# Down projections of a SwiGLU feed-forward as seven block products, with the block products chained in PSUM banks

## The chip, the cores and the metric

The kernel runs on one core of one Trainium2 chip. The metric is the device time of one execution in microseconds (us), given as the median of several runs. The profile is of one execution.

## The reference

Two layers of a decoder trunk over 512 tokens of 1024 features, all in fp32; the change concerns the feed-forward of both layers, where 2816 hidden features are 22 chunks of 128.

```python
def swiglu_ffn(h, w_gate_up, w_down):
    gu = h @ w_gate_up
    gate, up = gu[..., :D_FF], gu[..., D_FF:]
    return (jax.nn.silu(gate) * up) @ w_down

def reference(...):
    for i in range(DEPTH):                      # DEPTH = 2
        if i % N_MIXERS == 0:
            x = x + dilated_attention_mixer(rmsnorm(x, attn_norm[j]), w_qkv[j], w_attn_out[j])
        else:
            x = x + pooling_mixer(rmsnorm(x, pool_norm[j]), w_pool_in[j], w_pool_group[j], pool_scale[j])
        x = x + swiglu_ffn(rmsnorm(x, ffn_norm[i]), w_ffn_gate_up[i], w_ffn_down[i])
    return rmsnorm(x, final_norm)
```

## The kernel before

**Layout.** The residual stream is held transposed as eight tiles `X[0]` to `X[7]` of 128 features x 512 tokens. A product of a 128x128 weight block with such a tile is a matmul of 512 columns (one PSUM bank); with half the tokens it has 256 columns.

**Precision.** Each fp32 product is three matmuls: an operand is split into a high and a low part (`split`: ACT copies the high part, DVE subtracts it to get the low one), and the kernel adds high x high, high x low and low x high. Lines L254, L255 and L257 are these three in a plain product (class `Product`), L371, L372 and L373 in a block product (`mult`). Weights are split as well: tiles `whi`/`wlo` (or `halfhi`/`halflo`) come from a `raw` tile that a DMA filled, on L77 (ACT) and L78 (DVE).

**Block products.** For 17 of the 22 chunks of a feed-forward, gate and up together are one product of 2x2 blocks: the two block rows of the result are gate and up, the block columns are the two halves of the tokens, and the inner dimension is cut in two. Seven products of blocks stand in for eight (Strassen in Winograd's form), named "11", "1", "2", "21", "3", "22" and "4" after the operand of the tokens; each is 4 times 3 matmuls of 256 columns. Function `seven` runs them, each into a bank half of its own, and DVE adds the parts up (L412, L420, L425, L426). The first five chunks (`NPLAIN`) are plain pairs, while the operands of the tokens (`prepare`, `normed`) are still being made. The sums of weight blocks that a block product needs are made per chunk from three SP loads (L134, L135, L136), an accumulating DMA on POOL's queue (L137) and two DVE additions (L150, L151); class `Pair` does it.

**Down.** A feed-forward goes in two halves of 11 chunks (`HALF`). After each half, eight plain products of 11 chunks, one per output tile `m`, are added to `X[m]` (L954, or L879 in the second half of layer 0, which writes in the token order of layer 1). Their weights are 768 and 640 columns wide (`DOWN`). The last two tiles of layer 1 are made by halves of the tokens (`end`, `add`, `emit`, L1055 to L1072), with the final norm behind.

**Order.** Instructions are issued in the order in which the program writes them. Weights go through queues in the order of use: `loads` (DMAs), `steps` (splits) and `units`; `pump` issues the next of each when a buffer of the rings `BUFS` is free, and is called behind each product. PSUM has eight banks in rotation under one name, `ps`.

Of the kernel before, what the change touches and what calls it, by code (L numbers as in the profile page):

```python
# [15 lines left out]
P = 128  # L16
# [6 lines left out]
HALF = FC // 2  # L23
# [15 lines left out]
DOWN = (6, 5)  # L39
# [3 lines left out]
SLOTS = 15  # L43
# [5 lines left out]
def trunk(ctx: ExitStack, tc: tile.TileContext, xT, norms, w_first, w_qk, w_qkp, w_v0, w_v0p, w_v12, w_out, w_pair, w_down, w_pin, w_pgrp,  # L49
# [5 lines left out]
    psum = ctx.enter_context(tc.tile_pool(name="psum", bufs=8, space=PSUM))  # L55
# [10 lines left out]
    def ps():  # L66
        return psum.tile([P, S], F32, tag="ps", name="ps")


# [51 lines left out]
    class Pair:  # L121
# [3 lines left out]
        def __init__(self, src):  # L125
            self.src, self.w = src, {}
            loads.append((self, {"raw": 2, "rawhalf": 1}, self.load))
# [4 lines left out]
        def load(self):  # L132
            self.a, self.b, self.c = Held("raw"), Held("raw"), Held("rawhalf")
            nc.sync.dma_start(self.b.t, self.src[:, :2 * S])  # L134
            nc.sync.dma_start(self.a.t, self.src[:, S:3 * S])  # L135
            nc.sync.dma_start(self.c.t, self.src[:, :S])  # L136
            nc.gpsimd.dma_start(self.b.t.rearrange("p (a c) -> p a c", a=2),  # L137
                                self.src[:, None, 3 * S:].to_broadcast([P, 2, S]), accum_op=OP.add)

        def blocks(self):  # L140
            self.w["b"] = Held("w")
            split(*self.w["b"].t, self.a.t)

        def sums(self):
            self.w["s"] = Held("w")
            split(*self.w["s"].t, self.b.t)

        def more(self):
            a, b = self.a.t, self.b.t
            nc.vector.tensor_add(a[:, :S], a[:, :S], b[:, :S])  # L150
            nc.vector.tensor_add(a[:, S:], a[:, S:], a[:, :S])  # L151
            self.b.done()
            self.w["m"] = Held("w")
            split(*self.w["m"].t, a)
            self.a.done()

        def last(self):
            self.w["l"] = Held("half")
            split(*self.w["l"].t, self.c.t)
            self.c.done()  # L160
# [44 lines left out]
    def ffn_plan(layer):  # L205
        for hf in range(2):
            for j in range(hf * HALF, (hf + 1) * HALF):
# [4 lines left out]
            for m in range(KC):  # L212
                src = w_down[layer, hf, m]
                plain(src[:, :DOWN[0] * P], src[:, DOWN[0] * P:])
# [11 lines left out]
    class Product:  # L226


        def __init__(self, n, ins, w=None, keep=None):
# [935 lines left out]
```

## Time and profile before

| | us |
|---|---|
| median of 3 runs | 1267.53 (1267.21 to 1268.39) |
| span of the profiled execution | 1264.5 |
| PE busy | 1250.9 (99%), 8382 matmuls |
| PE weight loads | 1156.7 (91%) |
| DVE busy | 926.3 (73%) |
| ACT busy | 571.5 (45%) |
| POOL busy | 130.1 (10%) |

The mean granted TensorE clock is 0.998. The engines are PE (TensorE), PEld (its weight loads), DVE (VectorE), ACT (ScalarE), POOL (GpSimd) and SP (SyncE, which issues DMAs). An L with a number is a line of the program. A row for one instruction has its start from the beginning of the span, its duration, engine, line, operation, tiles (written <- read), shape and, in brackets, how long the engine was idle before it and what released it. A row for a group has a count, busy time and mean duration in ns, then the idle time ahead of the group and what ended it. Matmuls overlap, so their durations add up to more than the time they take.

### The profile page before, as it was taken

To read this page: it belongs to the slowest core of one execution; us is meant where nothing else is said; L and a number is where in the kernel's file an instruction comes from. 1 tells how busy PE (TensorE), PEld (TensorE's weight loads), DVE (VectorE), ACT (ScalarE), POOL (GpSimd) and SP (SyncE) were. 2 spreads that over 40 slices of the span, in tenths; PEclk is the share of its full clock that TensorE was granted. 3 is DMA by queue.
4 is the path that set the end of the run, shared out by engine and by line. 5 is a ranking of instruction groups with operands and counts; after the bars stand their busy time and mean duration, and the time that the engine had idled before them with its cause. 6 is when DMAs were issued, how large, how long until landed. Compare 5 with 4: busy or idle time off the path is not lost.

```text
span 1264.5 us, 21069 instructions
## 1 busy us (share of the span) xinstructions
PE 1250.9 (99%) x8382; PEld 1156.7 (91%) x8382; DVE 926.3 (73%) x1395; ACT 571.5 (45%) x885; POOL 130.1 (10%) x123
## 2 busy tenths in 40 slices
PE   9999999999999999999999999999999999999997
PEld 7889999999999988899989999888789988999987
DVE  6987788878778845689636887558978953788643
ACT  6445554545445543445324554343444532455331
POOL 1011111212111000110001110000301000110000
PEclk9999999999999999999999999999999999999999
DMA  8336556655756433256456774333135645676322
GB/s 295 101 95 164 130 157 145 162 139 144 182 137 152 139 133 120 67 129 181 124 146 158 181 188 126 97 133 130 37 95 123 175 126 142 168 182 173 93 69 67
DMA packets 67875, 174.04 MB, mean 138 GB/s; under 512 B 6960, under 2 KB 9152, under 8 KB 67776
## 3 DMA queue, kind: packets, MB, share of 16 engines
q1 hardware_dynamic: 48816, 136.49, 33.3%
q0 software_dynamic: 17808, 35.14, 16.4%
q8 instruction: 66, 1.08, 0.3%
q10 hardware_dynamic: 1152, 1.05, 0.2%
q14 instruction: 33, 0.27, 0.1%
HBM read 170.56 MB, written 2.10 MB: 137 GB/s over the span
## 4 chain that ended last, share of the span: by engine, by line
PE 75%; issue 12%; DVE 10%; ACT 1%; POOL 1%; DMA 0%; DVEq 0%; POOLq 0%
PE ps L372 13%; PE ps L371 13%; PE ps L373 13%; PE ps L254 8%; PE ps L255 8%; PE ps L257 8%; PE ps L483 2%; PE ps L484 2%; PE ps L485 2%; DVE wlo L78 2%; PE ps L678 1%; PE ps L590 1%; DVE raw L434 1%; POOL rcol L323 1%; PE ps L656 1%
## 5 line engine op out<-in xcount | busy, mean ns | idle before, releaser
L77 ACT ACTIVATE whi<-raw 128x1024 fp32r<-128x1024 f32 (+2 forms) x299 | 298.1, 1002 | 428.2 <-PE ps L255 198.4
L78 DVE TENSOR_TENSOR wlo<-raw,whi 128x1024 fp32r<-128x1024 f32 (+2 forms) x299 | 343.2, 1152 | 158.6 <-ACT whi L77 157.4
L254 PE MATMUL ps<-a,whi 128*128 128x512 f32 (+1 forms) x374 | 141.0, 377 | 0.0
L255 PE MATMUL ps<-a,whi 128*128 128x512 f32 (+1 forms) x374 | 140.9, 377 | 0.0
L257 PE MATMUL ps<-a,wlo 128*128 128x512 f32 (+1 forms) x374 | 140.8, 377 | 0.0
L371 PE MATMUL ps<-tt,whi 128*128 128x256 f32 x408 | 115.5, 283 | 0.0
L372 PE MATMUL ps<-tt,whi 128*128 128x256 f32 x408 | 115.5, 283 | 0.0
L373 PE MATMUL ps<-tt,wlo 128*128 128x256 f32 x408 | 115.5, 283 | 0.0
L137 POOL DMA_DIRECT2D raw<-w_pair x34 | 41.1, 1209 | 440.8 <-DMA raw<-w_pair 152.6
L257 PEld LDWEIGHTS ps<-a,wlo 128*128 128x128 f32 x374 | 70.4, 188 | 13.0
L254 PEld LDWEIGHTS ps<-a,whi 128*128 128x128 f32 x374 | 70.4, 188 | 12.8
L255 PEld LDWEIGHTS ps<-a,whi 128*128 128x128 f32 x374 | 70.4, 188 | 12.7
L371 PEld LDWEIGHTS ps<-tt,whi 128*128 128x128 f32 x408 | 78.3, 192 | 0.0
L372 PEld LDWEIGHTS ps<-tt,whi 128*128 128x128 f32 x408 | 78.3, 192 | 0.0
L373 PEld LDWEIGHTS ps<-tt,wlo 128*128 128x128 f32 x408 | 78.3, 192 | 0.0
L372 PE MATMUL ps<-tb,whi 128*128 128x256 f32 x272 | 77.2, 284 | 0.1
L373 PE MATMUL ps<-tb,wlo 128*128 128x256 f32 x272 | 77.0, 283 | 0.0
L371 PE MATMUL ps<-tb,whi 128*128 128x256 f32 x272 | 76.9, 283 | 0.0
L371 PE MATMUL ps<-h,whi 128*128 128x256 f32 x252 | 72.7, 289 | 0.0
L373 PE MATMUL ps<-h,wlo 128*128 128x256 f32 x252 | 71.3, 283 | 0.0
L372 PE MATMUL ps<-h,whi 128*128 128x256 f32 x252 | 71.3, 283 | 0.0
L254 PE MATMUL ps<-h,whi 128*128 128x512 f32 x144 | 56.4, 392 | 0.0
(280 smaller groups left out, 3415.5 us busy)
## 6 DMA issues: line engine op xcount, KB each, us to landing
raw<-w_pair SPq DMA_DIRECT2D x78, 512.0 KB, 4.3
raw<-w_qkp SPq DMA_DIRECT2D x36, 512.0 KB, 4.7
raw<-w_pair POOLq DMA_DIRECT2D x34, 512.0 KB, 7.2
raw<-w_down SPq DMA_DIRECT2D x32, 384.0 KB, 3.1
raw<-w_down SPq DMA_DIRECT2D x32, 320.0 KB, 2.8
raw<-w_v SPq DMA_DIRECT2D x18, 512.0 KB, 3.9
raw<-w_qkp POOLq DMA_DIRECT2D x18, 512.0 KB, 7.3
rawhalf<-w_pair SPq DMA_DIRECT2D x34, 256.0 KB, 3.5
```

The lines of the kernel that those rows point to most:

```text
L77: nc.scalar.activation(hi, v, AF.Copy)
L78: nc.vector.tensor_tensor(lo, v, hi.bitcast(F32), op=OP.subtract)
L137: nc.gpsimd.dma_start(self.b.t.rearrange("p (a c) -> p a c", a=2), self.src[:, None, 3 * S:].to_broadcast([P, 2, S]), accum_op=OP.add)
L254: nc.tensor.matmul(self.p[:, cols], w[0][:, s], mh[:, cols], start=self.done == 0, stop=False)
L255: nc.tensor.matmul(self.p[:, cols], w[0][:, s], ml[:, cols], start=False, stop=False)
L257: nc.tensor.matmul(self.p[:, cols], w[1][:, s], mh[:, cols], start=False, stop=self.done == self.n)
L371: nc.tensor.matmul(dst, w.t[0][:, c], th, start=k == 0, stop=False)
L372: nc.tensor.matmul(dst, w.t[0][:, c], tl, start=False, stop=False)
L373: nc.tensor.matmul(dst, w.t[1][:, c], th, start=False, stop=k == K2 - 1)
L483: nc.tensor.matmul(o, mh, wh, start=k == 0, stop=False)
L484: nc.tensor.matmul(o, mh, wl, start=False, stop=False)
L485: nc.tensor.matmul(o, ml, wh, start=False, stop=k == K2 - 1)
```

## The change

1. **Down as block products.** 20 of the 22 chunks go through down projections made as seven block products, in three groups: after chunks 0 to 7, 8 to 13 and 14 to 19 (`GROUPS`). A group has four of them (`down(g, i)`), one for each pair of output tiles `X[2i]`, `X[2i+1]`. Their products are of 4, 3 and 3 times 3 matmuls of 256 columns. The gate/up work of one more chunk is issued ahead of groups 0 and 1. Their weight blocks come through `Pair`, now for any width, from matrices that the host has cut into blocks (`down_blocks`).
2. **The last two chunks** stay plain products, two output tiles per weight unit (`last_plain`); block products of the last group and plain turns alternate by `TURNS`.
3. **Chains.** All block products of the feed-forwards now run in `chain` and no longer in `seven`: bank c takes "11", then "2", "3" and "4" on top; d starts as a copy of c after "11" and takes "21"; e starts as a copy of c after "2" and takes "22". "1" has a bank of its own. Five callbacks read the results (`share`, `left`, `high`, `right`, `low`). ACT makes the copies (L463, L471).
4. **Blocks of the hidden activation.** `half_of` and `blocks_of` turn the activations of two chunks into seven operands, with subtractions and splits on DVE and ACT (L989, L1004, L1005, L1012), two pieces behind each product of a chain from the fourth on (`some`). `up` is negated where it is written, and the sums into `X` change signs.
5. **Banks.** After the attention the eight banks are 3 `ps`, 3 `seed` (d, e) and 2 `sum` (c); plain products alternate between `ps` and `seed` (`full`). During the attention the three names rotate through all eight. There is one more slot for activations (`SLOTS` 16), and working tiles come from pools of their own.
6. **The end.** In layer 1 the last plain turns, for `X[4]` to `X[7]`, are made by halves of the tokens (L1243, L1248, L1259). The squares for the norms are summed in one tile in place (L306 to L310).

The next rows are DVE's in the first half of layer 0's feed-forward, from one gate/up block product to the next, before (`first` and `sums` are scratch tiles of `seven`, `a` the split activation):

```order
L412 TENSOR_TENSOR gt<-ps,first 128x512
L78 TENSOR_TENSOR wlo<-raw,whi 128x1024 x2
L420 TENSOR_TENSOR sums<-ps,gt 128x512
L78 TENSOR_TENSOR wlo<-raw,whi 128x1024
L425 TENSOR_TENSOR up<-ps,sums 128x512
L426 TENSOR_TENSOR gt<-sums,ps 128x256
L150 TENSOR_TENSOR raw<-raw 128x512
L78 TENSOR_TENSOR halflo<-rawhalf,halfhi 128x512
L866 TENSOR_TENSOR up<-up,gt 128x512
L151 TENSOR_TENSOR raw<-raw 128x512
L78 TENSOR_TENSOR a<-up,a 128x512
```

The same place in the changed kernel, on DVE (`hx` and `t` hold blocks of the hidden activation; L1072 is `high`, L1066 is `right`):

```order
L967 TENSOR_TENSOR hid<-up,gt 128x512
L173 TENSOR_TENSOR raw<-raw 128x512
L97 TENSOR_TENSOR hx<-hid,hx 128x256
L174 TENSOR_TENSOR raw<-raw 128x512
L989 TENSOR_TENSOR t<-hid 128x256
L97 TENSOR_TENSOR halflo<-rawhalf,halfhi 128x512
L97 TENSOR_TENSOR hx<-t,hx 128x256
L97 TENSOR_TENSOR wlo<-raw,whi 128x1024
L1072 TENSOR_TENSOR up<-sum,half 128x256
L97 TENSOR_TENSOR wlo<-raw,whi 128x1024
L1066 TENSOR_TENSOR gt<-seed,half 128x256
L97 TENSOR_TENSOR wlo<-raw,whi 128x1024
```

Four evacuations of up to 512 columns became two of 256, the blocks of the hidden activation came in, and one `wlo` now stands right ahead of `high`.

On DVE in layer 0's first down projections, before, the sums into `x` alternate with weight splits:

```order
L954 TENSOR_TENSOR x<-x,ps 128x512
L78 TENSOR_TENSOR wlo<-raw,whi 128x640
L954 TENSOR_TENSOR x<-x,ps 128x512
L78 TENSOR_TENSOR wlo<-raw,whi 128x768
L78 TENSOR_TENSOR wlo<-raw,whi 128x640
L954 TENSOR_TENSOR x<-x,ps 128x512
```

In the changed kernel DVE has this over one down chain of group 1 in layer 0 (L1080 and L1081 are `share`, L1084 `left`, L1087 `high`, L1085 `right`, L1086 `low`):

```order
L173 TENSOR_TENSOR raw<-raw 128x384
L97 TENSOR_TENSOR halflo<-rawhalf,halfhi 128x384
L1080 TENSOR_TENSOR x<-x,ps 128x256
L1081 TENSOR_TENSOR x<-x,ps 128x256
L174 TENSOR_TENSOR raw<-raw 128x384
L1084 TENSOR_TENSOR x<-x,seed 128x256
L97 TENSOR_TENSOR wlo<-raw,whi 128x768
L1087 TENSOR_TENSOR x<-x,sum 128x256
L97 TENSOR_TENSOR wlo<-raw,whi 128x768
L1085 TENSOR_TENSOR x<-x,seed 128x256
L97 TENSOR_TENSOR wlo<-raw,whi 128x768
L1086 TENSOR_TENSOR x<-x,sum 128x256
```

A chain makes two output tiles with six sums of 256 columns, and the additions for its weight blocks are new here; again a `wlo` stands ahead of `high`.

On PE, the end of a gate/up block product of layer 0 before: "22" into one bank, then "4" into another (bank names with their numbers):

```order
L371 MATMUL ps_6707<-tn_5901,whi_6609 128x256
L372 MATMUL ps_6707<-tn_5901,whi_6609 128x256
L373 MATMUL ps_6707<-tn_5901,wlo_6610 128x256
L371 MATMUL ps_6706<-tt_5749,halfhi_6629 128x256
L372 MATMUL ps_6706<-tt_5749,halfhi_6629 128x256
```

The same place in a down chain of the changed kernel, with sum_8020 this chain's bank c, which "3" wrote and `high` reads, seed_8023 its bank e, and sum_8120 the next chain's c:

```order
L389 MATMUL seed_8023<-hy_7847,whi_7967 128x256
L390 MATMUL seed_8023<-hy_7847,whi_7967 128x256
L391 MATMUL seed_8023<-hy_7847,wlo_7968 128x256
L389 MATMUL sum_8120<-hx_7173,whi_8002 128x256
L389 MATMUL sum_8020<-hu_7332,halfhi_7981 128x256
L390 MATMUL sum_8020<-hu_7332,halfhi_7981 128x256
```

"4" now goes to the bank that "3" had, and one matmul of the next chain stands ahead of it.

The diff, cut to its core:

```diff
-HALF = FC // 2
+GROUPS = ((0, 8), (8, 14), (14, 20))
+LAST = FC - GROUPS[-1][1]
+TURNS = (("block", 0), ("block", 1), ("plain", 0), ("block", 2), ("plain", 1), ("block", 3), ("plain", 2), ("plain", 3))
-DOWN = (6, 5)
-SLOTS = 15
+SLOTS = 16
+RING = ("ps", "seed", "sum", "ps", "seed", "sum", "ps", "seed")
+BANKS = {"ps": 3, "seed": 3, "sum": 2}
...
+    def chain(T, share, left, right, low, high, behind=None):
+        unit, = units.popleft()
+        n = unit.q // P
+        c, a, d, e = (ps(tag)[:, :H2] for tag in ("sum", "ps", "seed", "seed"))
+        ...
+        def step():
+            pump()
+            i = next(turns)
+            if behind:
+                behind(i)
+
+        wb = part(unit, "b")
+        mult(c, wb, 0, T, "11", n=n)
+        nc.scalar.copy(d, c)
+        step()
+        ws = part(unit, "s")
+        mult(a, ws, 0, T, "1", n=n)
+        share(a)
+        step()
+        wm = part(unit, "m")
+        mult(c, wm, 0, T, "2", True, n=n)
+        nc.scalar.copy(e, c)
+        step()
+        mult(d, wb, 1, T, "21", True, n=n)
+        wb.done()
+        left(d)
+        step()
+        mult(c, ws, 1, T, "3", True, n=n)
+        ws.done()
+        high(c)
+        step()
+        mult(e, wm, 1, T, "22", True, n=n)
+        wm.done()
+        right(e)
+        step()
+        wl = part(unit, "l")
+        mult(c, wl, 0, T, "4", True, n=n)
+        wl.done()
+        low(c)
+        step()
...
+            def some(i):
+                for n in range(2 if i > 2 else 0):
+                    if pieces:
+                        pieces.popleft()()
+
+            def strassen_pair(j):
+                ...
+                def right(p):
+                    nc.vector.tensor_sub(gt[:, hi], p, half)
+                    nc.scalar.activation(gt[:, hi], gt[:, hi], AF.Silu)
+
+                chain(T, lambda p: nc.scalar.copy(half, p),
+                      lambda p: nc.scalar.activation(gt[:, lo], p, AF.Silu), right,
+                      lambda p: nc.scalar.copy(up[:, lo], p),
+                      lambda p: nc.vector.tensor_sub(up[:, hi], p, half), some)
+                hide(j, gt, up)
+
+            def down(g, i):
+                x1, x2 = X[2 * i], X[2 * i + 1]
+
+                def share(p):
+                    nc.vector.tensor_add(x1[:, hi], x1[:, hi], p)
+                    nc.vector.tensor_sub(x2[:, hi], x2[:, hi], p)
+
+                chain(TH[g], share,
+                      lambda p: nc.vector.tensor_sub(x1[:, lo], x1[:, lo], p),
+                      lambda p: nc.vector.tensor_sub(x1[:, hi], x1[:, hi], p),
+                      lambda p: nc.vector.tensor_add(x2[:, lo], x2[:, lo], p),
+                      lambda p: nc.vector.tensor_add(x2[:, hi], x2[:, hi], p))
...
-            for hf in range(2):
-                ...
-                for m in range(KC - 2 if nxt == 4 and hf else KC):
-                    ...
-                        nc.vector.tensor_add(X[m], X[m], f.p)
+            for g, (first, stop) in enumerate(GROUPS):
+                for j in range(first + (g > 0), stop + 1 if g < 2 else FC):
+                    if j < NPLAIN:
+                        plain_pair(j)
+                        if j < K2:
+                            prepare(j)
+                    else:
+                        strassen_pair(j)
+                if g < 2:
+                    while len(pieces) > 2:
+                        pieces.popleft()()
+                    for i in range(K2):
+                        down(g, i)
+                    drop("hb")
+            ...
+            for kind, i in TURNS[:-2] if layer else TURNS:
+                if kind == "block":
+                    down(2, i)
+                else:
+                    last_plain(i)
...
+            for m in range(K2, KC):
+                sq = add(m, 0, end(m, 0))
+            add(4, 1, end(4, 1))
+            r = rstd([sums[0], sq])
+            add(5, 1, end(5, 1))
+            add(6, 1, end(6, 1))
+            pr = spread(r)
+            f = end(7, 1)
+            emit(0, pr, range(2))
+            sq = add(7, 1, f)
+            r = rstd([sums[1], sq])
+            ...
+            emit(0, pr, range(2, KC))
+            ...
+            emit(1, pr, range(KC), spare, row)
```

More of the change, by code (lines that the diff above doesn't have):

```diff
@@ L923, in prepare @@
[L923 to L935 removed]
+                T["22", k] = cut(two(T["n"], k % 2), b22)
+                give(("hp", k))
+                give(("tp", k))
@@ L1145 @@
         "w_pair": pair,
-        "w_down": dn,
+        "w_down": down,
+        **{f"w_down{g}": down_blocks(*span) for g, span in enumerate(GROUPS)},
         "w_pin": tiled(v["w_pool_in"][0]),
```

504 lines of the change are left out of this document (285 added, 219 removed).

## Prediction

> **What bounds the kernel now.** I read the page's engine table and slices first, then busy time by stage over the first feed-forward layer, then single instructions in it. The page:
>
> ```profile
> span 1264.5 us, 21069 instructions
> PE 1250.9 (99%) x8382; PEld 1156.7 (91%) x8382; DVE 926.3 (73%) x1395; ACT 571.5 (45%) x885; POOL 130.1 (10%) x123
> ...
> PE   9999999999999999999999999999999999999997
> PEld 7889999999999988899989999888789988999987
> DVE  6987788878778845689636887558978953788643
> ```
>
> TensorE (PE) is busy in every slice but the last, and no other engine is. The stages of layer 0's feed-forward (columns: PE, PEld, DVE, ACT, POOL busy, then granted clock, DMA share and GB/s) are plain pairs, gate/up block products, down projections, gate/up again, a mixed stretch, down projections:
>
> ```profile
> 509.00:553.70 44.70, 44.57 (x200) 36.70 (x200) 38.10 (x58) 20.65 (x31) 4.49 (x3) 1.00 0.33 82
> 553.70:625.00 71.30, 71.25 (x552) 69.19 (x551) 57.35 (x83) 34.00 (x50) 4.82 (x4) 1.00 0.61 162
> 625.00:665.00 40.00, 40.00 (x178) 33.15 (x177) 15.77 (x20) 10.08 (x12) 2.41 (x2) 1.00 0.49 133
> 665.00:760.00 95.00, 95.00 (x757) 93.37 (x756) 77.34 (x104) 47.01 (x61) 10.86 (x9) 1.00 0.68 175
> 760.00:820.00 60.00, 60.00 (x366) 54.01 (x366) 38.44 (x58) 25.11 (x36) 0.00 (x0) 1.00 0.37 114
> 820.00:857.00 37.00, 37.00 (x169) 30.80 (x168) 18.96 (x23) 15.28 (x21) 0.00 (x0) 1.00 0.37 128
> ```
>
> PE never pauses there, at full clock; DVE has 19% free beside block products and 61% in the down stage. So time is the sum of PE's issue intervals, and the change is worth what it takes off them, less every wait it makes. Durations overlap, so I take intervals between starts, 76 of each kind:
>
> ```profile
> 489.81 0.39 PE L255 MATMUL ps<-oh,whi 128*128 128x512 f32 x1
> ...
> 507.03 0.39 PE L257 MATMUL ps<-h,wlo 128*128 128x512 f32 x1
> ```
> ```profile
> 749.74 0.28 PE L372 MATMUL ps<-tt,whi 128*128 128x256 f32 x1
> ...
> 758.86 0.28 PE L373 MATMUL ps<-tt,wlo 128*128 128x256 f32 x1
> ```
>
> 17.22/76 = 0.2266 us for 512 columns, 9.12/76 = 0.1200 for 256. Two halves cost 0.240, 6% more than a whole: an eighth fewer products saves 1 - 0.875 x 0.240/0.2266 = 7.3%.
>
> **The matmuls.** By the two programs' order, 512-column matmuls go from 2238 to 1320, 256-column ones from 5454 to 7050 (840 more per layer in twelve down blocks; 132 at the old end become 48). 1596 x 0.1200 = 191.5 in, 918 x 0.2266 = 208.0 out: -16.5 us.
>
> The two sizes' weight loads take nearly the same:
>
> ```profile
> L254 PEld LDWEIGHTS ps<-a,whi 128*128 128x128 f32 x374 | 70.4, 188 | 12.8
> L371 PEld LDWEIGHTS ps<-tt,whi 128*128 128x128 f32 x408 | 78.3, 192 | 0.0
> ```
>
> The Trainium skill ("TensorE: Matmul & The Clock Gate", Back-to-back issue gap and LDWEIGHTS) gives 518 and 262 cycles at 2.4 GHz for isolated gaps and about 107 ns for a load; that would make the term 1596 x 0.109 - 918 x 0.216 = -24.3, an estimate by that page. The trace disagrees at both sizes (0.2266 and 0.1200; loads of 188 and 192 ns), so the measured -16.5 stands.
>
> **The hand-off inside a chain.** Where the old block product gave each partial sum its bank half and evacuated later, the chain adds into one bank c: ACT copies c to d and e, then "3" adds onto c, DVE reads c out (`high`), "22" runs, and "4" adds onto c again. PE waits if `high` is not done within "22", 12 matmuls (1.44 us) in gate/up and group 0, 9 (1.08) in groups 1 and 2. Ahead of `high` in DVE's queue stands `wlo` of the next middle matrices, whose `whi` on ACT reuses the buffer that "21" has just finished with. The rows for that loop:
>
> ```profile
> 710.14 0.28 PE L372 MATMUL ps<-tt,whi 128*128 128x256 f32 x1
> 710.26 0.28 PE L373 MATMUL ps<-tt,wlo 128*128 128x256 f32 x1
> ```
> ```profile
> 710.46 1.06 ACT L77 ACTIVATE whi<-raw 128x1024 fp32r<-128x1024 f32 x1 [1.30 <-PE ps L372]
> ```
> ```profile
> 703.21 0.68 DVE L150 TENSOR_TENSOR raw<-raw 128x512 f32<-128x512 f32 x1
> 703.81 0.69 DVE L420 TENSOR_TENSOR sums<-ps,gt 128x512 f32<-128x512 f32 x1
> 704.41 1.22 DVE L78 TENSOR_TENSOR wlo<-raw,whi 128x1024 fp32r<-128x1024 f32 x1
> 705.55 0.68 DVE L425 TENSOR_TENSOR up<-ps,sums 128x512 f32<-128x512 f32 x1
> 706.15 0.41 DVE L426 TENSOR_TENSOR gt<-sums,ps 128x256 f32<-128x256 f32 x1
> 706.48 0.68 DVE L151 TENSOR_TENSOR raw<-raw 128x512 f32<-128x512 f32 x1
> ...
> 711.55 1.23 DVE L78 TENSOR_TENSOR wlo<-raw,whi 128x1024 fp32r<-128x1024 f32 x1 [1.05 <-ACT whi L77]
> ```
> ```profile
> 554.39 0.69 DVE L78 TENSOR_TENSOR tb<-raw,tb 128x512 fp32r<-128x512 f32 x1
> ...
> 555.14 0.19 PEld L372 LDWEIGHTS ps<-tb,whi 128*128 128x128 f32 x1 [0.26 <-DVE tb L78]
> ```
> ```profile
> L77 ACT ACTIVATE whi<-raw 128x768 fp32r<-128x768 f32 x32 | 27.1, 846 | 66.6 <-PE ps L255 53.5 <-PE ps L372 11.4 <-issue 1.8
> ```
>
> From these: `whi` starts 0.32 after the start of the last reader of its buffer, takes 1.06 (768 columns: 0.85), `wlo` follows 0.03 after; DVE instructions queued back to back start 1.14 apart for 1024 columns, 0.60 for 512, 0.33 for 256, so about 0.87 for 768; a weight load starts 0.06 after the DVE end it waits for, 0.12 ahead of its matmul. With t = 0 at the first matmul of "22", the last reader in "21" starts at -1.68. Gate/up: `whi` -1.36 to -0.30, `wlo` from -0.27, `high` 0.87 to 1.28 (0.41), load free at 1.34; due at 1.32: 0.02 late. Groups 1 and 2: reader at -1.32, `whi` -1.00 to -0.15, `wlo` from -0.12, `high` 0.75 to 1.16, free at 1.22; due, with the one matmul of the next chain that the order puts ahead, at 1.08: 0.14 late. There are 34 gate/up chains and 8 of group 0 (x 0.02 = 0.8), and 15 of 16 in groups 1 and 2 with such a split ahead (x 0.14 = 2.1): +2.9 us. Ends: 0 (the order already hides some), and 58 x 0.2 = 11.6 if a short DVE instruction is usually in the way.
>
> DVE keeps up on paper. A gate/up chain now queues three 1024 splits, six or so of 512, two reads of c and e, and the blocks of the hidden activation: 7.5 us for an even chunk, 9.0 for an odd one, of 10.08. A down chain of three pairs has 3 x 0.87 + 3 x 0.47 + 6 x 0.33 = 6.0 of 7.56; 7.2 when it prepares gate/up weights. ACT takes over 5 or 6 short copies (about 0.3 each) and goes to some 7 of 10.08. The copies c to d and c to e have a whole further product to finish in: nothing for them.
>
> **Into the block products.** Hidden blocks of the five plain pairs pile up and come two per step, eight in the first chain. I count 7.8 us of DVE work from that chain's start to the end of its `high` read, due at 8.6; DVE arrives about 1 us behind, because the plain stage rises to some 94% of 44 us. 2 layers x 0.7 = +1.4; ends 0 and 4.
>
> **Out of layer 0.** Its last two plain turns, X[4..7], take 4 x 1.36 us on PE, where a tile was 7.5 before; each needs an unfolding subtraction, a scaled remainder and a square sum on DVE.
>
> ```profile
> L879 DVE TENSOR_TENSOR x<-x,ps 128x512 f32<-128x512 f32 x7 | 7.8, 1115 | 9.7 <-PE ps L257 9.7
> ```
>
> About 1.03 + 0.66 + 0.60 = 2.3 us a tile, plus pooling weight splits: tile 5's operand is ready 8.5 us after the last block, PE wants it at 7.9; tile 6 0.3 late; and the last block's chain inherits 0.5 of lag. +1.3; ends 0 and 4.
>
> **The end.** Before:
>
> ```profile
> 1254.15 0.28 PE L257 MATMUL ps<-a,wlo 128*128 128x256 f32 x1
> ```
> ```profile
> 1254.92 0.42 ACT L1057 ACTIVATE sq<-x 128x256 f32<-128x256 f32 x1 [3.18 <-DVE x L1055]
> ```
> ```profile
> 1257.85 2.44 DVE L1072 SCALAR_TENSOR_TENSOR x<-x,nrm,ps 128x256 f32<-128x256 f32 x6 [1.58 <-PE ps L331]
> ```
>
> 10.2 us lie from the last down matmul's issue end (1254.27) to the span's end. After it, PE finishes eight pieces of 0.72 us, too short to cover the first half's eight scaled outputs, and DVE reads tile 7 behind two of them. Following DVE's queue from the last block, the final square ends at 9.1 us and the span at 18.3, of which 7.1 is PE work: a tail of 11.2, +1.0. Ends -0.5 and 3.
>
> Attention keeps its order (the three bank names rotate through the same eight banks), DMA bytes for down weights grow by about 16 MB but at the block stage's 182 GB/s per PE time, so both cost nothing while the buffers are full.
>
> **Sum.** -16.5 + 2.9 + 1.4 + 1.3 + 1.0 = -9.9 on a span of 1264.5, so 1254.6; the median of the runs lies 3.0 above that span, and I keep that difference: 1267.5 - 9.9 = **1257.6 us**.
>
> **Rivals.** (1) Slower: `high` is late in every chain. For it: 0.02 is no margin, and one more 256-column instruction (0.33) ahead of it suffices. Against: DVE has a tenth or more of each chain free. Without the hand-off term the gain is 12.8 us, so it decides from 12.8/58 = 0.22 us a chain; at 0.33, 1267.5 - 12.8 + 19.1 = 1273.8. The Trainium skill ("Perfetto Trace Analysis", Optimizing Tensor Performance) says independent matmul groups should rotate through different PSUM banks and larger matmuls are more efficient; the chain goes against both. No run here shows that wait yet.
>
> (2) Late weights in groups 1 and 2. A block's first raw buffer comes free with `L173`; before, the load left 1.85 us after the same add (703.81), and its accumulation 4.4 later:
>
> ```profile
> 705.66 0.33 SPq L134 DMA_DIRECT2D raw<-w_pair  x1
> ```
> ```profile
> 710.04 1.20 POOL L137 DMA_DIRECT2D raw<-w_pair  x1 [8.73 <-DVE wlo L78]
> ```
> ```profile
> raw<-w_pair POOLq DMA_DIRECT2D x34, 512.0 KB, 7.2
> ```
>
> With 7.2 to land that is 13.4 us, where a chain of 7.56 leaves about 12.1. ACT then waits on the transfer with the copy c to d queued behind. Against: blocks of three quarters the size, and 1.5 us of slack before that copy is due. At 0.5 us in 16 chains: 1257.6 + 8 = 1265.6, no change.
>
> (3) No new wait at all, the order covering each: 1267.5 - 16.5 + 0.5 = 1251.5.
>
> (4) A short matmul costs half a long one, 0.2266/2 = 0.1133, because the new products run in longer unbroken sequences than the old: 1596 x 0.1133 - 208.0 = -27.2, 10.7 below my term, so 1246.9. Against it stand 5454 short matmuls already in long sequences at 0.1200. The TensorE page's gaps, cited above, would give 1249.8 by the estimate there.
>
> **How the numbers follow.** My case (1252.5 to 1264.5): 0.70. Rival 1: 0.09; rival 2: 0.09, half of it within 0.2%; rival 3: 0.11; rival 4: 0.01. A difference of 0.2% (2.5 us) is about what this measurement tells from none. Faster: 0.70 + 0.12 and a little of rival 2 = 0.84; same 0.06; slower 0.10. The range runs from just under rival 3, 1251.0, to the upper end of my case, 1264.5; it leaves out rivals 1, 4 and most of 2, under 2 in 10.
>
> **What would show it.** Right: PE without gaps inside gate/up chains, starts 0.120 apart in the down stages, gaps of 0.1 to 0.2 at "4" in groups 1 and 2, DVE near 85% in both stages, a tail of about 11 us. Wrong: PE's weight loads waiting on `L1072` or `L1087` for 0.3 us or more in most chains, ACT's `whi` waiting on `w_down` transfers, or a busy DVE with PE idle over the first two block chains.

## The result and the profile after

| | before | after |
|---|---|---|
| median, us | 1267.37 (1267.14 to 1268.39, 4 runs) | 1256.8 (1255.83 to 1257.1, 4 runs) |
| ratio | | 0.9915, 95% interval 0.9901 to 0.9929 |
| span of the profiled execution, us | 1264.5 | 1254.1 |

The kernel became 0.85% faster, 10.6 us; the forecast was 1257.6. The page of the changed kernel:

```profile
span 1254.1 us, 23222 instructions
PE 1237.9 (99%) x9060; PEld 1172.9 (94%) x9060; DVE 1012.5 (81%) x1687; ACT 680.2 (54%) x1171; POOL 157.4 (13%) x147
...
PE   9999999999999999999999999999999999999996
```

PE still bounds; DVE went from 73% to 81%, ACT from 45% to 54%. By stage (columns as before: stretch, its length, then PE, PEld, DVE, ACT and POOL busy, granted clock, DMA share, GB/s) there are layer 0's first gate/up chains, its gate/up before group 1, group 1, its last gate/up, the turns of group 2; then layer 1's last gate/up, and the end behind the last down matmul:

```profile
553.30:593.51 40.21, 40.19 (x337) 39.99 (x336) 36.45 (x63) 28.64 (x53) 4.82 (x4) 1.00 0.61 154
...
633.79:693.84 60.05, 60.05 (x506) 60.02 (x505) 48.01 (x80) 39.24 (x72) 7.25 (x6) 1.00 0.73 174
693.84:725.17 31.33, 31.33 (x259) 30.86 (x258) 26.90 (x50) 16.21 (x26) 3.61 (x3) 1.00 0.75 187
725.17:796.47 71.30, 70.08 (x585) 69.56 (x584) 55.79 (x91) 46.12 (x84) 8.43 (x7) 1.00 0.68 172
796.47:838.80 42.33, 41.86 (x302) 38.87 (x301) 38.35 (x65) 24.75 (x41) 2.41 (x2) 1.00 0.60 174
...
1127.48:1196.98 69.50, 69.50 (x585) 69.47 (x584) 55.60 (x91) 45.68 (x83) 8.43 (x7) 1.00 0.71 172
1240.43:1254.06 13.63, 3.86 (x18) 3.23 (x16) 6.18 (x17) 0.80 (x2) 2.10 (x3) 0.60 0.47 155
```

The same end before, behind the last down matmul:

```profile
1254.27:1264.50 10.23, 2.26 (x18) 1.90 (x16) 3.18 (x9) 0.80 (x2) 2.11 (x3) 0.69 0.46 155
```

The reader is to see three things: gate/up and down run on PE without a hole (60.05 of 60.05, 31.33 of 31.33) at 80% and 86% of DVE; layer 0's last gate/up is 1.8 us longer than the same stage of layer 1; and the end is 3.4 us longer than before, in these two profiles. Cut at the same places, the spans differ like this:

| stretch | before | after | difference |
|---|---|---|---|
| to the first plain pair | 497.06 | 496.62 | -0.4 |
| plain pairs of layer 0 | 56.67 | 56.68 | 0.0 |
| layer 0, block products and down | 291.39 | 285.50 | -5.9 |
| pooling layer, plain pairs of layer 1 | 115.57 | 116.85 | +1.3 |
| layer 1, block products and down | 293.58 | 284.78 | -8.8 |
| end | 10.23 | 13.63 | +3.4 |

**The hand-off** is the wait that was forecast. PE and DVE in a gate/up chain of layer 0 (L1072 is `high`, the rows with halfhi are "4"):

```profile
641.85 0.42 DVE L1072 TENSOR_TENSOR up<-sum,half 128x256 f32<-128x256 f32 x1
642.22 0.28 PE L391 MATMUL seed<-tn,wlo 128*128 128x256 f32 x1
642.33 0.38 PE L389 MATMUL sum<-tt,halfhi 128*128 128x256 f32 x1
642.54 0.28 PE L390 MATMUL sum<-tt,halfhi 128*128 128x256 f32 x1
```

and in a down chain of group 1 (L1087 is `high`):

```profile
707.66 0.41 DVE L1087 TENSOR_TENSOR x<-x,sum 128x256 f32<-128x256 f32 x1
707.81 0.28 PE L391 MATMUL seed<-hy,wlo 128*128 128x256 f32 x1
707.93 0.28 PE L389 MATMUL sum<-hx,whi 128*128 128x256 f32 x1
708.13 0.38 PE L389 MATMUL sum<-hu,halfhi 128*128 128x256 f32 x1
708.36 0.28 PE L390 MATMUL sum<-hu,halfhi 128*128 128x256 f32 x1
```

DVE's reading ends at 642.27 and 708.07, PE's row starts 0.06 behind it, and the first two steps take 0.32 where two ordinary ones take 0.24, in the second case 0.43. Over all 58 chains I add up the start intervals there above an ordinary one: 0 to 0.09 in most chains of gate/up and group 0, 0.13 to 0.23 in nearly all of groups 1 and 2, together 5.0 us.

**The pitch**, the interval from one matmul's start to the next, changed too, which nothing in the forecast had. From the first to the last of 60 matmuls of a gate/up chain in the changed kernel, and of 25 matmuls of 512 columns in the pooling layer:

```profile
655.28 0.28 PE L389 MATMUL ps<-tt,whi 128*128 128x256 f32 x1
...
662.29 0.28 PE L391 MATMUL seed<-tn,wlo 128*128 128x256 f32 x1
```
```profile
856.20 0.40 PE L273 MATMUL ps<-h,whi 128*128 128x512 f32 x1
...
861.76 0.40 PE L273 MATMUL seed<-h,whi 128*128 128x512 f32 x1
```

7.01/59 = 0.1188 us where it was 0.1200, and 5.56/24 = 0.232 where it was 0.2266; over all of them behind layer 0's plain pairs 0.1188 and 0.2305.

### The profile page after: what moved, and what is told of

Read it like the earlier page. It is cut to its first block, busy times and chain, and to the rows that moved or that the text cites. A ratio compares the mean times of both kernels' runs of the same rounds, so it can differ in the third digit from the quotient of the medians.

```text
span 1254.1 us, 23222 instructions
## 1 busy us (share of the span) xinstructions
PE 1237.9 (99%) x9060; PEld 1172.9 (94%) x9060; DVE 1012.5 (81%) x1687; ACT 680.2 (54%) x1171; POOL 157.4 (13%) x147
## 3 DMA queue, kind: packets, MB, share of 16 engines
q8 instruction: 71, 1.16, 0.4%
## 5 line engine op out<-in xcount | busy, mean ns | idle before, releaser
L389 PE MATMUL sum<-tt,whi 128*128 128x256 f32 x272 | 76.9, 283 | 1.2 <-ACT seed L471 0.8
L390 PE MATMUL sum<-tt,whi 128*128 128x256 f32 x272 | 76.6, 281 | 0.0
L391 PE MATMUL sum<-tt,wlo 128*128 128x256 f32 x272 | 76.4, 281 | 0.0
L96 ACT ACTIVATE halfhi<-rawhalf 128x512 fp32r<-128x512 f32 (+1 forms) x87 | 53.2, 612 | 20.0 <-PE sum L390 12.7
L173 DVE TENSOR_TENSOR raw<-raw 128x512 f32<-128x512 f32 (+1 forms) x87 | 57.5, 661 | 2.5 <-issue 2.4
L174 DVE TENSOR_TENSOR raw<-raw 128x512 f32<-128x512 f32 (+1 forms) x87 | 57.5, 661 | 0.2
L97 DVE TENSOR_TENSOR halflo<-rawhalf,halfhi 128x512 fp32r<-128x512 f32 (+1 forms) x87 | 57.4, 661 | 0.0
L389 PEld LDWEIGHTS sum<-tt,whi 128*128 128x128 f32 x272 | 51.3, 189 | 1.6 <-ACT seed L471 1.0
L471 ACT COPY seed<-sum 128x256 f32<-128x256 f32 x58 | 20.8, 359 | 57.9 <-PE sum L391 57.8
L390 PEld LDWEIGHTS sum<-tt,whi 128*128 128x128 f32 x272 | 51.2, 188 | 0.0
L391 PEld LDWEIGHTS sum<-tt,wlo 128*128 128x128 f32 x272 | 51.2, 188 | 0.0
L389 PE MATMUL sum<-hz,whi 128*128 128x256 f32 x160 | 45.4, 284 | 0.5 <-ACT seed L471 0.3
L390 PE MATMUL sum<-hz,whi 128*128 128x256 f32 x160 | 45.2, 283 | 0.0
L390 PE MATMUL seed<-hy,whi 128*128 128x256 f32 x160 | 45.2, 282 | 0.0
L391 PE MATMUL seed<-hy,wlo 128*128 128x256 f32 x160 | 45.1, 282 | 0.0
L389 PE MATMUL seed<-hy,whi 128*128 128x256 f32 x160 | 45.0, 281 | 0.0
```

The costliest lines, as they stand in the source:

```text
L96: nc.scalar.activation(hi, v, AF.Copy)
L97: nc.vector.tensor_tensor(lo, v, hi.bitcast(F32), op=OP.subtract)
L173: nc.vector.tensor_add(a[:, :q], a[:, :q], b[:, :q])
L174: nc.vector.tensor_add(a[:, q:2 * q], a[:, q:2 * q], a[:, :q])
L389: nc.tensor.matmul(dst, w.t[0][:, c], th, start=k == 0 and not onto, stop=False, skip_group_check=onto)
L390: nc.tensor.matmul(dst, w.t[0][:, c], tl, start=False, stop=False, skip_group_check=onto)
```

## The experiments

Each kernel is the changed one with one edit, but for e9_both, which has two, and e12_before, which is the kernel before with its two padding tiles left out. Times are compared by the ratio to the kernel before in the same job (its medians there: 1267.12, 1267.43 and 1267.43), and stages by the profiles.

### e1_tail: an output DMA moved off ACT

```diff
-                    (nc.scalar if k % 2 else nc.sync).dma_start(outT[k, :, cols], y)
+                    (nc.scalar if k % 2 and (half or k > 1) else nc.sync).dma_start(outT[k, :, cols], y)
```

> One output DMA of the first token half (k = 1) is issued by SP's queue instead of ACT's; nothing else changes. In the changed kernel that DMA's issue stands on ACT from 1241.37 for 1.30 us, and the final square, whose input is done at 1241.66, starts at 1242.77. Theory A (that issue delays the final square, and everything behind it): the square starts about 1.05 us earlier, and the span ends 0.9 to 1.1 us earlier, some 1255.8 against 1256.8. Rival (DVE's scaled outputs of the first half and the last norm set the end anyway): within 0.3 us of the changed kernel.

1254.89 us, ratio 0.9907 (0.9893 to 0.9920); the end behind the last down matmul took 11.3 us instead of 13.63 in the profile. In the changed kernel, DVE's last update of X, ACT's issue of the DMA, the final square, and PE's matmuls for the norm, with a window of which the third number from the end is PE's granted clock:

```profile
1241.25 0.41 DVE L1243 TENSOR_TENSOR x<-x,ps 128x256 f32<-128x256 f32 x1
1241.37 1.30 ACTq L1260 DMA_DIRECT2D outT<-x  x1
1242.77 0.42 ACT L1245 ACTIVATE sq<-x 128x256 f32<-128x256 f32 x1 [2.38 <-DVE x L1259]
1243.24 1.01 PE L335 MATMUL ps<-ones,sq 128*128 128x1 f32 x4 [1.64 <-ACT sq L1245]
1245.35 2.08 PE L348 MATMUL ps<-ident,rcol 128*128 128x128 f32 x8 [1.10 <-POOL rcol L340]
...
1243.00:1245.00 2.00, 1.01 (x4) 0.93 (x4) 0.64 (x3) 0.19 (x1) 0.40 (x1) 0.53 0.57 189
```

and with the DMA on SP:

```profile
1242.08 0.41 DVE L1243 TENSOR_TENSOR x<-x,ps 128x256 f32<-128x256 f32 x1
...
1242.59 0.42 ACT L1245 ACTIVATE sq<-x 128x256 f32<-128x256 f32 x1 [1.36 <-DVE x L1243]
1243.06 0.61 PE L335 MATMUL ps<-ones,sq 128*128 128x1 f32 x4 [0.62 <-ACT sq L1245]
1244.76 1.16 PE L348 MATMUL ps<-ident,rcol 128*128 128x128 f32 x8 [1.10 <-POOL rcol L340]
...
1243.00:1245.00 2.00, 0.84 (x6) 0.76 (x7) 1.51 (x5) 0.00 (x1) 0.70 (x1) 1.00 0.59 197
```

From DVE's update to the square 1.52 us became 0.51, as theory A has it. The rest of the 2.35 is the clock: in the changed kernel it is at 0.53 and 0.50 when the norm's small matmuls run, and they take 1.01 and 2.08 us, here 0.61 and 1.16 at 1.00.

How much of this one can count on is not shown, for both parts vary without any edit there. Nine kernels, the changed one and eight of these, have the same code at the end, with this DMA on ACT. Its issue takes 0.37 or 0.38 us in four of their profiles and 1.10 to 1.37 in five (why is open), and their ends take 11.7 to 13.6 us. In e6_twice (below), with an end of 11.73:

```profile
1246.18 0.38 ACTq L1264 DMA_DIRECT2D outT<-x  x1
1246.66 0.42 ACT L1249 ACTIVATE sq<-x 128x256 f32<-128x256 f32 x1 [1.45 <-DVE x L1247]
```

The clock is at 1.00 for 1239.04 us and then falls, in the changed kernel as in e1_tail; in the other traces the full clock lasts as long, or 1235.62, 1242.45 or 1252.69 us, always whole multiples of one step of 3.41. It rose 4.08 us into the span in the changed kernel and 6.83 in e1_tail, so it falls 2.7 us behind the last down matmul here and 4.6 there; in e5_ownbank, whose square is as late as the changed kernel's, it falls at 4.8. So how much of its 1.3 us is due to the edit, and how much to where the steps lay in these two executions, is open. The Trainium skill ("TensorE: Matmul & The Clock Gate", Part 1) says that PE's clock falls to half after an idle window of about 3.4 us, and that the window does not start with the kernel. The traces agree with the half and with the step; but PE was not idle in the 3.41 us ahead of this fall, with 0.61 us of matmuls from 1241.00 on. Between the two kernels' times the intervals overlap.

### e3_shift, e8_place, e11_apart, e12_before: where the operands lie

```diff
-        fpool.tile([P, 32], F32, name="shift", bufs=1)
```

That is e3_shift. Fixed slots are the buffers for activations that exist from the start, late slots those made after the attention (pool `fpool`, where this padding tile lies). e11_apart makes the tile 64 columns wide; e8_place drops it and puts a tile of 32 columns ahead of all slots and weights; e12_before drops it and the other padding tile (in `tmp`) from the kernel before.

> A 128-byte padding tile ahead of the activation slots is left out, so that the slots which lie at multiples of 512 bytes in the changed kernel lie 384 bytes past one, where all of them and all weight tiles lay in the kernel before. Order and instructions are the same. Theory A (the matmul pitch depends on where the operands lie): 256-column matmuls of the feed-forward go back from 0.1187 to 0.1200 us, 512-column ones from 0.2293 to 0.2267, and about 4550 x 1.3 ns - 360 x 2.6 ns = 5 us are lost: some 1262. Rival (the pitch comes with the chains, not with addresses): pitches stay 0.1187 and 0.2293, time within 0.5 us of the changed kernel.

> All activation slots, fixed and late ones, and all weight tiles lie at multiples of 512 bytes (a padding tile moves from the late pool to the front); order and instructions are those of the changed kernel, in which the fixed slots and the weights lie 384 bytes past a multiple and the late slots at one. Theory A (what counts is where the tokens' operand lies): 256-column matmuls at 0.1187 us or less in the feed-forwards and now also in the attention, about 2500 x 1.3 ns = 3 us faster than the changed kernel, plain ones of 512 columns at 0.2293 everywhere, 500 x 2.6 ns = 1.3 us back. Theory B (what counts is that tokens' operand and weights lie alike or apart within 512 bytes): all alike again, 0.1200 and 0.2267 as in the kernel before and in e3_shift, some 1259.

> The late activation slots lie 128 bytes past a multiple of 512, the fixed slots and the weight tiles 384 past one as in the changed kernel; nothing else changes. In the kernel before and in e3_shift and e8_place, with all of them alike, the feed-forward's pitches are 0.1200 and 0.2267; in the changed kernel, with the late slots at a multiple, 0.1187 and 0.2293. Theory A (unlike places among slots and weights count): 0.119 and 0.229 here, within 1 us of the changed kernel. Theory B (only slots at a multiple of 512 count): 0.1200 and 0.2267 as with all alike, about 2.5 us slower.

> The kernel before, with the two padding tiles left out, so that its late slots lie at multiples of 512 bytes and its fixed slots and weights 384 past one, as in the changed kernel. Theory A (the pitch is the place's, whatever the products are): the 2856 gate/up matmuls of 256 columns go from 0.1200 to 0.1187 (3.7 us less), some 1400 of 512 columns after the attention from 0.2267 to 0.2293 (3.6 us more), so the time stays within 1.5 us of the kernel before, with both pitches changed in its profile. Theory B (it takes the chains or the changed pools): pitches 0.1200 and 0.2267 as before, time the same.

| kernel | late slots | fixed slots | weights | 256 columns | 512 columns | ratio |
|---|---|---|---|---|---|---|
| before | 384 | 384 | 384 | 0.1200 | 0.2269 | 1 |
| changed | 0 | 384 | 384 | 0.1188 | 0.2305 | 0.9915 (0.9901 to 0.9929) |
| e3_shift | 384 | 384 | 384 | 0.1200 | 0.2277 | 0.9938 (0.9925 to 0.9950) |
| e8_place | 0 | 0 | 0 | 0.1200 | 0.2278 | 0.9931 (0.9918 to 0.9943) |
| e11_apart | 128 | 384 | 384 | 0.1200 | 0.2277 | 0.9941 (0.9928 to 0.9955) |
| e12_before | 0 | 384 | 384 | 0.1187 | 0.2305 | 1.0005 (0.9996 to 1.0014) |

The three columns of places are bytes past a multiple of 512 in the built programs; the pitches are means in us over all steps of a size behind layer 0's plain pairs, steps with a wait left out. In e3_shift 47 steps of a chain take 5.64 us, 0.1200 each; in e12_before, the old block products and the old down products run over 101 and 86 steps from

```profile
720.01 0.28 PE L371 MATMUL ps<-tt,whi 128*128 128x256 f32 x1
...
731.98 0.28 PE L370 MATMUL ps<-tn,whi 128*128 128x256 f32 x1
```
```profile
640.17 0.39 PE L256 MATMUL ps<-a,wlo 128*128 128x512 f32 x1
...
659.86 0.39 PE L254 MATMUL ps<-a,whi 128*128 128x512 f32 x1
```

to 0.1185 and 0.2290. So the pitch belongs to the places and not to the chains: the kernel before shows it as soon as its late slots lie like the changed kernel's, and there the shorter steps of one size pay for the longer ones of the other (ratio 1.0005). e11_apart's theory A fell: unlike places alone don't do it. e8_place's theory A fell for the feed-forwards; in its attention the steps of 256 columns went from 0.1198 to 0.1191 in the mean. There not all lies alike: the attention's tiles `tx` are 128 bytes past a multiple in every kernel, 256 bytes from the weights' places in the other five and 128 from them here.

One description fits the steps of 256 columns in all twelve stretches, attention and feed-forwards of the six kernels. Where slots, these tiles and weights all lie alike modulo 256 bytes, as 384 and 128 do, the mean is 0.1198 to 0.1200. Where some of them lie 128 apart, it is 0.1187 to 0.1191, also for the steps whose own two operands lie alike. The 512-column steps are 0.2305 in the two kernels that mix such places in the feed-forwards and 0.2269 to 0.2278 in the others. No run was made to test this, and why it is so stays open. Comparing the changed kernel with e3_shift by stage, its place is worth 3.1 us in the stages from the first block products to the end of down, and costs 0.7 in the pooling layer: 2.4 net, about half of what e3_shift's theory A had, in part because hand-offs are shorter at the longer pitch (3.5 us for 5.0).

### e5_ownbank: no hand-off

```diff
-        mult(c, wl, 0, T, "4", True, n=n)
+        f = ps("ps")[:, :H2]
+        mult(f, wl, 0, T, "4", n=n)
         wl.done()
-        low(c)
+        low(f)
```

> In every chain the product 4 goes to a bank of its own, so that it waits for no reading of bank c; the adding of 3 to it is left out, so the result lacks that part. Theory A (the gaps at the start of 4, about 0.05 us in gate/up and group 0 and 0.17 in groups 1 and 2, 5.0 us over 58 chains, are the wait for DVE's reading of c): the gaps vanish and the time falls by 4 to 5 us, to about 1252.3. Rival (they are the price of a new weight tile or of the turn itself): gaps and time stay. Third possibility: the gaps vanish, but the wait moves to the next thing that DVE delivers, and less than 2 us are won.

1253.85 us, ratio 0.9896 (0.9883 to 0.9910). None of the 58 gaps is left, so they were the wait for `high`. But by the profiles only about 1.3 us of the 5.0 remain in the stages with chains: the third possibility, though what PE now waits for is ACT and not DVE. (By the ratios 2.4 us are won, with intervals that overlap.) Cut at equal numbers of matmuls, every other stage with chains got shorter by 0.2 to 0.4 us and group 1 by 0.65, but the last gate/up stages of both layers grew by 1.1 and 1.3, with waits of 0.5 to 1.2 us for ACT's copies c to d and c to e. PE arrives earlier at weights that don't.

### e10_noacc: fewer transfers around group 1

```diff
-            nc.gpsimd.dma_start(b.rearrange("p (a c) -> p a c", a=2),
-                                self.src[:, None, 3 * q:].to_broadcast([P, 2, q]), accum_op=OP.add)
+            if q == S or self.src.shape[-1] == 4 * S:
+                nc.gpsimd.dma_start(b.rearrange("p (a c) -> p a c", a=2),
+                                    self.src[:, None, 3 * q:].to_broadcast([P, 2, q]), accum_op=OP.add)
```

> The 16 accumulating DMAs of POOL's queue for the down blocks of groups 1 and 2 are left out, so one of the four loads of each such block is missing and the result lacks that part; matmuls and splits are as in the changed kernel. In the changed kernel, e1_tail, e5_ownbank, e6_twice and e8_place alike, the first gate/up products after group 1 of layer 0 have waits of 0.6 to 1.2 us for ACT's copies c to d and c to e, with ACT 2.4 us on the transfer of raw w_pair before; layer 1 has none or shorter ones. Theory A (the transfers of that stretch, a DMA share of 0.74 to 0.79, come late, and the copies stand behind the split that waits for them): with 16 transfers fewer the waits vanish, the stage goes from 71.3 to 69.5, some 1255. Rival (the order on ACT and DVE makes them, a cut of the hidden activation ahead of the copy c to e): the waits stay, within 0.5 us of the changed kernel.

1256.59 us, ratio 0.9914 (0.9900 to 0.9927), the time of the rival; layer 0's stage went from 71.3 to 70.9 and layer 1's from 69.5 to 70.7. The two waits in the changed kernel, with an accumulating transfer on POOL's queue, ACT's splits, the copies (L463, L471) and the matmuls that wait for them:

```profile
717.91 1.20 POOL L158 DMA_DIRECT2D raw<-w_pair  x1 [8.60 <-ACT halfhi L96]
...
726.13 1.06 ACT L96 ACTIVATE whi<-raw 128x1024 fp32r<-128x1024 f32 x1 [2.42 <-DMA raw<-w_pair]
...
727.61 0.37 ACT L463 COPY seed<-sum 128x256 f32<-128x256 f32 x1
728.03 0.39 PE L389 MATMUL sum<-tt,whi 128*128 128x256 f32 x1 [0.43 <-ACT seed L463]
...
735.60 1.06 ACT L96 ACTIVATE whi<-raw 128x1024 fp32r<-128x1024 f32 x1 [2.00 <-PE sum L391]
...
741.03 0.63 ACT L96 ACTIVATE hz<-t 128x512 fp32r<-128x512 f32 x1 [1.58 <-DVE t L1005]
741.57 0.37 ACT L471 COPY seed<-sum 128x256 f32<-128x256 f32 x1
741.99 0.39 PE L389 MATMUL sum<-tt,whi 128*128 128x256 f32 x1 [0.78 <-ACT seed L471]
```

With 16 accumulations fewer the first wait is gone, the second is there in both layers (0.95 each), again behind a late transfer:

```profile
735.92 1.06 ACT L96 ACTIVATE whi<-raw 128x1024 fp32r<-128x1024 f32 x1 [2.32 <-DMA raw<-w_pair]
...
741.35 0.63 ACT L96 ACTIVATE hz<-t 128x512 fp32r<-128x512 f32 x1 [1.58 <-DVE t L1006]
741.89 0.37 ACT L472 COPY seed<-sum 128x256 f32<-128x256 f32 x1
```

The split that waits holds up its own DVE half and so the cuts of the hidden activation; ACT waits for such a cut with the copy c to e behind it. What the split waits for is the accumulating transfer of its gate/up block: it starts 0.16 us behind that landing each time. The one issued at 717.91 took 8.05 us to land, and the next one, for the split at 735.60, took 7.59. In layer 1 of the changed kernel, which has neither wait, they took 6.66 and 6.93. In e10_noacc the first took 6.60 in layer 0 and 6.77 in layer 1, the second 8.64 and 8.28. So theory A's mechanism, a late transfer with copies behind the split that waits for it, is there, but its remedy helps the first of the two alone: they are accumulations of gate/up blocks, which stay. Why they take so long in this stretch is open; those of groups 1 and 2 alone are not the reason.

### e6_twice: `high` made longer

```diff
         ws.done()
+        nc.vector.tensor_copy(spare, c)
         high(c)
```

> Before `high` DVE copies bank c once more into a spare tile (256 columns), in all 58 chains; nothing else changes. It doubles the suspected wait: 4 may write c only after both readings. A queued DVE instruction of 256 columns takes 0.33 us. Theory A (the hand-off has no slack: its gaps of 0.05 and 0.17 us are the end of that reading): each gap grows by about 0.33, 58 x 0.33 = 19 us, some 1276, as in the slower case of the prediction. Rival (the reading is done in time and the gap is a fixed cost of turning to a bank again): under 5 us slower.

1259.42 us, ratio 0.9938 (0.9924 to 0.9951): 2.6 us slower than the changed kernel, not 19. The gaps grew from 5.0 to 10.2 us in all, 0.09 a chain. In a gate/up chain of layer 0:

```profile
653.51 0.42 DVE L480 COPY spare<-sum 128x256 f32<-128x256 f32 x1
653.84 0.41 DVE L1074 TENSOR_TENSOR up<-sum,half 128x256 f32<-128x256 f32 x1
653.92 0.28 PE L391 MATMUL seed<-tn,wlo 128*128 128x256 f32 x1
654.04 0.28 PE L389 MATMUL sum<-tb,whi 128*128 128x256 f32 x1
654.16 0.28 PE L390 MATMUL sum<-tb,whi 128*128 128x256 f32 x1
654.31 0.39 PE L389 MATMUL sum<-tt,halfhi 128*128 128x256 f32 x1
```

DVE did take 0.33 longer, but PE's order is not the one written: two matmuls of the next chain's "11" (the rows with tb) now stand ahead of "4" and cover most of it. The order is fixed when the program is built; the longer reading was seen there, and filled. Neither theory had that; the wait has no slack, as A says, and the time moves as little as the rival says.

### e4_seven, e7_seven, e9_both: gate/up without chains

```diff
             def strassen_pair(j):
-                chain(T, ...)
+                p1, p26, p45, p73 = (ps(tag) for tag in ("seed", "ps", "sum", "ps"))
+                mult(p1[:, :H2], w, 0, T, "11")
+                nc.scalar.copy(first, p1[:, :H2])
+                mult(p26[:, :H2], w, 1, T, "21")
+                ...
+                nc.vector.tensor_add(gt, p26, again(first))
+                mult(p73[:, H2:], w, 1, T, "22")
+                nc.vector.tensor_add(sums, p73[:, :H2], gt[:, hi])
+                ...
```

e4_seven took the banks in rotation over all three names.

> The 34 gate/up block products run again as in the kernel before (four banks, parts added up by DVE behind the matmuls), the down projections stay block products in chains. Theory A (gate/up needed the chains because of DVE): DVE gets three evacuations of up to 512 columns for two of 256, about 1.6 us more a chunk, on 48 of 60 us that it is busy now, so 9.7 of each 10.08 us; odd chunks, which cut three pieces, go over, and PE waits: 3 us slower than the changed kernel (0 to 10), some 1260. Rival 1 (the chain's hand-off is what costs): the 34 hand-offs of about 0.05 us are gone and DVE still fits, 1.7 us faster. Rival 2 (the shorter pitch of 0.1187 belongs to the chains): pitch back to 0.1200 in gate/up only, 34 x 84 x 1.3 ns = 3.7 us slower with no waits on DVE.

> Gate/up by the four-bank block products of the kernel before, as in e4_seven, but in the banks ps and sum (and one of seed), so that all is computed; down in chains. Theory A (e4_seven's time holds: DVE keeps up with the wider evacuations, the 34 hand-offs of about 0.045 us are gone, and so are the 1.5 us of late copies c to d and c to e in layer 0's last gate/up stage, since no matmul waits for ACT there): 2.5 to 3.5 us faster than the changed kernel, some 1253.8. Rival (with fewer banks to rotate, DVE's 9.7 us a chunk shows): 0 to 5 us slower than the changed kernel.

> e7_seven and e1_tail together: gate/up by four-bank block products, down in chains, and the output DMA of k = 1 not issued by ACT ahead of the final square. Theory A (the two are independent): e7_seven less 1.5 to 2.3 us, the tail's 2.35 us in e1_tail less what e7_seven's tail may already lack, some 1252. Rival (the tail then waits for DVE): as e7_seven.

e4_seven: 1253.73 us, ratio 0.9903 (0.9887 to 0.9918). Its bank rotation leaves part of the down chains' sums out; e7_seven, in other banks, leaves out nothing. The Trainium skill ("PSUM — Partial Sum Buffer", The four PSUM rules) has a rule for it: the first matmul of a group clears the written marks of its whole bank, not only of the columns it writes, and a later matmul that does not start a group overwrites where the mark is clear. By that rule a copy c to d or e is lost where an old product last started a group in the bank's other half; no run here reads the marks.

e7_seven: 1255.53 us, ratio 0.9909 (0.9894 to 0.9924); e9_both: 1254.51, ratio 0.9898 (0.9884 to 0.9911). Layer 0's first two gate/up stages in e7_seven:

```profile
553.50:593.37 39.87, 39.87 (x337) 39.86 (x336) 39.53 (x68) 24.00 (x36) 3.61 (x3) 1.00 0.61 157
633.61:693.42 59.81, 59.81 (x507) 59.81 (x505) 55.92 (x95) 32.48 (x48) 7.25 (x6) 1.00 0.73 176
```

DVE is busy 99% and 93.5% and PE still has no hole: e4_seven's theory A fell, DVE does keep up. Each gate/up stage is 0.2 to 0.3 us shorter than with chains, and layer 0's last one 2.1 (69.17 instead of 71.30), since no matmul there waits for ACT; 2.0 us come back in group 2's first chain, as waits of 0.87 for ACT's copy c to e and 1.01 for DVE's `high`. The pitch stays 0.1188, so rival 2 fell too. e7_seven's own theory A fell short: about 1 us faster than the changed kernel and not 2.5 to 3.5, for those 2.0 us. The whole gain of the change is there without chains in gate/up. In e9_both the end is 0.13 us shorter than e7_seven's, which was 1.6 shorter than the changed kernel's already: the rival's number, but not shown as its cause, since behind the last down matmul the final square comes 0.38 us earlier and the fall of PE's clock 0.9 earlier. It has the best ratio of the kernels that compute all, though its interval overlaps the changed kernel's.

## Why the prediction was right, point by point

The forecast lay 0.8 us from the median, but partly because errors of both signs met. Against the span's -10.4:

- **Matmuls, -16.5.** The counts hold, and so does the price at the old places: e3_shift has 0.1200. That a tile's place moves the pitch was not in the sum: -2.4 net (e3_shift against the changed kernel). Nothing in the working stands for it, so this part of the match is luck. The Trainium skill's gaps ("TensorE: Matmul & The Clock Gate", Back-to-back issue gap), which made this term -24.3 by estimate, stay off: the shorter steps of 0.1188 are still 9% above its 0.109.
- **Hand-off, +2.9.** Place and mechanism were right, the size a little low: 3.5 us at the forecast's pitch (e3_shift), where 0.02 late was 0.03 in the mean and 0.14 was 0.14. At the shorter pitch, which arrives earlier at the same DVE end, it is 5.0, with 0.05 and 0.17. The first chain of each layer, priced apart at 1.4 for both ("into the block products"), has 0.28 and 0.19 in that same sum: DVE was not a whole microsecond behind. This step was over-sized.
- **Rival 1** lost for a reason I did not have: e6_twice shows that a reading of 0.33 us more costs 0.09 a chain, because the order brings matmuls of the next chain forward.
- **Rival 2, late weights,** had the mechanism, the accumulating transfer, and missed the place: not in groups 1 and 2, but in the first two gate/up products behind group 1, 0.59 + 0.94 = 1.5 us in layer 0. Both are waits for the copies c to d and c to e, which the sum put at nothing because they have a whole further product to finish in. e5_ownbank shows that such waits limit what a faster PE could gain.
- **Out of layer 0, +1.3.** At the place named, the pooling layer's first operands, PE waits once, 0.42 us for ACT's `h` at 845.00, and waits further on in that layer are shorter than before. The rest is two waits of 0.33 and 0.48 for the copies c to d and c to e, behind plain turns of group 2, 0.8 us.
- **The end, +1.0.** Mis-sized in the profile: +3.4, just above the upper end of 3. The step that failed is "following DVE's queue": ACT's queue held an output DMA ahead of the final square (e1_tail), and PE's clock fell early. Both vary from profile to profile: with the same end, e6_twice and e7_seven, where the issue is short, have +1.5 and +1.8, and the old end takes 11.68 us in e12_before instead of 10.23. So the change itself may cost little more than was forecast; how much is open.

At the sizes measured in these profiles: -16.5 - 2.4 + 3.5 + 1.5 + 0.8 + 3.4 - 0.4 (attention, which differs by up to 1.1 between profiles of the same code) = -10.1, of -10.4.

## What to carry to other kernels

Where PE is busy throughout, price a change by start intervals times counts, then look for every place where PE takes up a bank that another engine still reads, and measure those few hundredths times their number. A DMA issue on an engine's queue is work in that queue: keep it from standing ahead of the last small step on which the end depends. Read such an end in more than one profile. And when two versions place their buffers differently, compare the pitch of an untouched instruction first, or the layout is taken for the algorithm.

## What the runs showed of the hardware

Padding that moved the late slots by 128 bytes moved the pitch of the matmuls in both kernels: 256 columns from 0.1200 to 0.1188 or 0.1187, 512 columns from 0.2269 to 0.2305, in opposite directions. Late slots at a multiple of 512 bytes with weights 384 past one gave it in two kernels; late slots at 384 or 128 past one with the same weights did not, nor, in the feed-forwards, everything at a multiple. In these rows it goes with operands that lie 128 bytes apart modulo 256. At the end PE's granted clock fell from 1.00 to 0.50 in a stretch with single small products, which made eight 128-column matmuls take 2.08 us instead of 1.16; the full clock had lasted a whole multiple of 3.41 us in every trace. The issue of one output DMA held ACT's queue for 0.37 us or for 1.10 to 1.37, in profiles of the same code.
